# A hybrid recurrent and attention block on one core: buffers, load order and one engine's work moved at five places

## The chip, the cores and the metric

The kernel runs on one core of a Trainium2 chip. The core has TensorE (PE, with PEld for its weight loads), VectorE (DVE), ScalarE (ACT), GpSimd (POOL) and SyncE (SP, which here only issues DMA). The metric is the device time of one execution in microseconds (us), the median of several.

## The reference

One layer, sequence 2048, width 1024, all in float32. From the normed and modulated input h come two branches, merged by gates and projected:

```python
h = rms_norm(x, g_norm) * (1 + scale) + shift          # shift, scale, gate from c
rnn_x, rnn_gate, q, k, v, attn_gate, g_rnn, g_attn = split(h @ w_in)   # eight parts of 1024
a = rg_lru(causal_conv(rnn_x)) * silu(rnn_gate)         # recurrence along the sequence
b = mixture([dilated_window_attention(rope(q), rope(k), v, w, d)
             for w, d in ((128, 1), (512, 4), (2048, 16))]) * silu(attn_gate)
merged = sigmoid(g_rnn) * (a @ w_out_rnn) + sigmoid(g_attn) * (b @ w_out_attn)
out = rms_norm(x + gate * (merged @ w_o), g_final)
```

The rotary angle acts on 32 of the 128 channels of each head ("rotated" rows); the other 96 are "plain".

## The kernel before

Every float32 operand is split into a high and a low part (`hi_act` on ScalarE, `lo_dve` or `lo_pool` on VectorE or GpSimd: low = value − high), and every product is three matmuls (`mm3`). A matmul of 128x512 is the unit nearly everywhere.

The sequence runs in two halves, f = 0 and 1. In each half the input projections are computed in pairs of tiles: `strassen` makes one pair from seven products of 12 matmuls, with weight combinations that are built in the first half, kept in DRAM (`sD`) and read back in the second. The combinations of partial products are kept in the tiles u1, u2 and u3 (u1 a copy by ScalarE, L384; u2 and u3 sums by VectorE, L385 and L390), which lie in the pool that the caller passes: `rp` while the recurrent and gate pairs run, `qp` while the rotated and plain q and k pairs run. `rp` closes when the former are done and `qp` takes its memory.

The order is written out by hand: after each product the functions due at that count run (`later(d, fn)` and `after_prod`, by `run_late`), under a manual schedule, so every engine's stream is in that order. Loads go out on SP, a few on ACT; raw weights pass through a ring R of five tiles (`raw_tile`), in which the weights of the first half, and in the second half those of the output projections, land and are split. In both halves `rotary_tables` builds cosines and sines in pieces: a repeat (L1020), four transposes on TensorE (L1025), a copy or a product (L1031), and a store to the DRAM tensor `tabD`; the repeat and the product use the tag `ev` of `rp`, three buffers, which the gate pairs use too. `load_tables` (L1053) brings them back at the start of `qp` as Ct and St. There, in the first half, `next_norm` loads the other half of x (L511) and squares it (L1240), and `next_even` builds the next operands.

Behind both halves come the attention of eight heads and, between its steps, the output projections' products ("fill"): job j, tile t = 8j + m, eight inputs k of 512 columns each, loaded by `load_y` and split by `split_y`. `at(s, place, fn)` puts a step of a head at a slot of the schedule; a head's queries and keys arrive by four calls of `load_kq` (L1368, L1369), are split by `split_kq` at slots of their own (`enlist`) and the queries are rounded (L1382). From t = 40 on (`TAIL0`), the final projection's operand B is also built on the side: `load_rows` brings rows of w_o, `gate_rows` (L1857) multiplies them by the residual gate, `high`, `low` and `combine` make the operands B11 to T4, in four blocks k by `build_rows`. Then the final product runs in pairs again, with the residual and the last norm behind it.

A DMA's completion is signalled by one of eight semaphores, taken in turn by SP and ACT (DMAHW0 to DMAHW7 in the listings below).

## Time and profile before

| | us |
|---|---|
| median of 3 runs | 2223.52 (2220.85 to 2224.8) |
| the profiled execution | 2226.09 |
| its span | 2224.3 |
| TensorE busy | 2170.7 (98%) |
| VectorE busy | 1443.0 (65%) |
| ScalarE busy | 1287.1 (58%) |
| GpSimd busy | 1027.7 (46%) |
| mean granted TensorE clock | 0.992 |

Times within the span are counted from its start. By them the first half's pairs in `rp` end near 595 us, its rotated and plain pairs near 700; the second half's near 1260 and 1377; attention runs to about 1914, the building of the final operand to about 2050. A row of the timeline is start, duration, engine, line, operation, output <- inputs, shape, count, and in brackets the engine's idle time before it and what ended it.

### The profile page before, as it was taken

To read this page: it belongs to the slowest core of one execution; us is meant where nothing else is said; L and a number is where in the kernel's file an instruction comes from. 1 tells how busy PE (TensorE), PEld (TensorE's weight loads), DVE (VectorE), ACT (ScalarE), POOL (GpSimd) and SP (SyncE) were. 2 spreads that over 40 slices of the span, in tenths; PEclk is the share of its full clock that TensorE was granted. 3 is DMA by queue.
4 is the path that set the end of the run, shared out by engine and by line. 5 is a ranking of instruction groups with operands and counts; after the bars stand their busy time and mean duration, and the time that the engine had idled before them with its cause. 6 is when DMAs were issued, how large, how long until landed. Compare 5 with 4: busy or idle time off the path is not lost.

```text
span 2224.3 us, 34201 instructions
## 1 busy us (share of the span) xinstructions
PE 2170.7 (98%) x11326; PEld 1836.2 (83%) x11326; DVE 1443.0 (65%) x2518; ACT 1287.1 (58%) x2570; POOL 1027.7 (46%) x764
## 2 busy tenths in 40 slices
PE   8999999999999999999999999999999999999998
PEld 5998888888777998888788887788888988887886
DVE  5838888878546715544435353466777777688787
ACT  6637678668543626557447311677888887433333
POOL 2457777667557422222223112455666664310443
PEclk9999999999999999999999999999999999999999
DMA  8367887887989468898888998877887886898543
GB/s 286 117 214 256 281 294 270 295 286 263 316 274 293 129 211 271 291 290 270 295 285 305 341 338 260 267 242 250 269 269 219 249 247 217 297 318 282 180 166 109
DMA packets 412278, 573.41 MB, mean 258 GB/s; under 512 B 72423, under 2 KB 270275, under 8 KB 411077
## 3 DMA queue, kind: packets, MB, share of 16 engines
q1 hardware_dynamic: 369892, 442.82, 63.5%
q10 hardware_dynamic: 42016, 128.36, 15.1%
q8 instruction: 90, 1.47, 0.3%
q14 instruction: 88, 0.71, 0.1%
q0 software_dynamic: 192, 0.05, 0.0%
HBM read 352.99 MB, written 218.11 MB: 257 GB/s over the span
## 4 chain that ended last, share of the span: by engine, by line
PE 53%; DMA 5%; issue 3%; DVE 3%; ACT 3%; POOL 2%; SPq 1%; ACTq 0%; POOLq 0%; DVEq 0%
PE pj L150 10%; PE X L150 10%; PE V L150 9%; PE W L150 5%; PE Z L150 5%; PE Y L150 4%; PE sc L150 3%; PE o L150 3%; PE pg L150 1%; PE pT L1505 1%; PE pT L1518 1%; ACT pp L1421 1%; DMA S<-wD 1%; POOL q L1382 1%; POOL kq L164 1%
## 5 line engine op out<-in xcount | busy, mean ns | idle before, releaser
L164 POOL TENSOR_TENSOR S<-R,S 128x512 fp32r<-128x512 f32 x168 | 257.8, 1542 | 170.4 <-ACT S L158 70.0
L150 PE MATMUL X<-T,S 128*128 128x512 f32 x1344 | 325.9, 391 | 6.3 <-ACT u L384 4.7
L150 PE MATMUL pj<-yh,S 128*128 128x512 f32 x896 | 327.2, 406 | 4.2 <-ACT yh L158 1.5
L150 PE MATMUL V<-T,S 128*128 128x512 f32 x1344 | 324.9, 391 | 2.3 <-DVE t L454 2.0
L150 PEld LDWEIGHTS X<-T,S 128*128 128x128 f32 x1344 | 252.5, 189 | 61.8 <-ACT u L384 6.5
L150 PEld LDWEIGHTS V<-T,S 128*128 128x128 f32 x1344 | 251.6, 188 | 57.6 <-DVE t L454 3.3
L150 PEld LDWEIGHTS pj<-yh,S 128*128 128x128 f32 x896 | 169.4, 189 | 36.1 <-DVE S L167 2.2
L164 POOL TENSOR_TENSOR S<-s,S 128x512 fp32r<-128x512 f32 x92 | 140.1, 1523 | 115.2 <-ACT S L158 69.1
L150 PE MATMUL pj<-yl,S 128*128 128x512 f32 x448 | 177.0, 395 | 3.2 <-DVE yl L167 3.0
L1421 ACT ACTIVATE pp<-pp,st 128x256 f32<-128x256 f32 (+3 forms) x256 | 133.5, 523 | 59.8 <-DVE st L1420 59.2
L150 PE MATMUL Y<-T,S 128*128 128x512 f32 x672 | 163.4, 392 | 0.0
L150 PE MATMUL Z<-T,S 128*128 128x512 f32 x672 | 161.9, 390 | 0.0
L150 PE MATMUL W<-T,S 128*128 128x512 f32 x672 | 161.7, 389 | 0.0
L150 PEld LDWEIGHTS Y<-T,S 128*128 128x128 f32 x672 | 127.0, 189 | 26.4
L150 PEld LDWEIGHTS W<-T,S 128*128 128x128 f32 x672 | 126.0, 188 | 27.0 <-issue 0.9
L167 DVE TENSOR_TENSOR ptl<-pT,pth 128x384 fp32r<-128x384 f32 (+1 forms) x160 | 97.9, 628 | 77.2 <-ACT pth L158 75.0
L150 PEld LDWEIGHTS Z<-T,S 128*128 128x128 f32 x672 | 125.9, 188 | 26.1
L164 POOL TENSOR_TENSOR s<-R,s 128x512 fp32r<-128x512 f32 x32 | 45.8, 1430 | 208.4 <-ACT s L158 161.8
L912 DVE SCALAR_TENSOR_TENSOR xc<-xr,par,xc 128x512 f32<-128x512 f32 x96 | 99.0, 1031 | 47.9 <-ACT xc L906 45.6
L158 ACT ACTIVATE S<-R 128x512 fp32r<-128x512 f32 x168 | 101.5, 622 | 46.8 <-DMA R<-in_w_in_dram 14.2
L1485 ACT ACTIVATE pp<-pp,M 128x256 f32<-128x256 f32 (+3 forms) x256 | 118.0, 523 | 9.7 <-DVE M L1608 9.7
L1420 DVE CUSTOM_DVE_ANT_0 pp<-sc,msk 128x256 f32<-128x256 f32 (+3 forms) x256 | 103.6, 448 | 29.0 <-PE sc L150 27.1
(416 smaller groups left out, 4927.1 us busy)
## 6 DMA issues: line engine op xcount, KB each, us to landing
sD<-S ACTq DMA_DIRECT2D x196, 512.0 KB, 4.2
S<-sD SPq DMA_DIRECT2D x196, 512.0 KB, 5.3
S<-wD SPq DMA_DIRECT2D x82, 512.0 KB, 5.3
R<-in_w_in_dram SPq DMA_DIRECT2D x136, 256.0 KB, 4.3
wD<-s ACTq DMA_DIRECT2D x64, 256.0 KB, 5.4
T<-in_w_mod_dram SPq DMA_DIRECT2D x8, 1024.0 KB, 11.7
vN<-ev SPq DMA_DIRECT2D x64, 128.0 KB, 2.8
zaT<-ev SPq DMA_DIRECT2D x32, 256.0 KB, 4.4
```

The lines of the kernel that those rows point to most:

```text
L150: nc.tensor.matmul(o, lhsT=l, rhs=r, start=st, stop=sp, **kw)
L158: nc.scalar.activation(o, i, AF.Copy)
L164: nc.gpsimd.tensor_tensor(o, i, h.bitcast(F32), ALU.subtract)
L167: return nc.vector.tensor_tensor(o, i, h.bitcast(F32), ALU.subtract).ins
L912: nc.vector.scalar_tensor_tensor(xc, xr[:, i : i + CH], cw(i), xc, ALU.mult, ALU.add)
L1382: nc.gpsimd.tensor_copy(t[:, l], src.rearrange("p r (b a) -> p b r a", b=4))
L1420: nc.vector.tensor_tensor_reduce(pdst, s_ps, mask, 1.0, 3e38, ALU.add, ALU.min, m_)
L1421: nc.scalar.activation(pdst, pdst, AF.Exp, bias=m_, scale=-1.0, accum_out=l_)
L1485: nc.scalar.activation(pp, pp, AF.Copy, scale=w)
L1505: nc.tensor.transpose(pt[:, c0 + j * P : c0 + (j + 1) * P], pp[i][:, k * P : (k + 1) * P], ident)
L1518: nc.tensor.transpose(pt[:, c * P : (c + 1) * P], pp[:, half * P : (half + 1) * P], ident)
```

## The change

Five edits. (1) u1, u2 and u3 lie in a pool `pu` that is opened before `rp` and closed after `qp`, in each half. With it the table loads, the x loads of `next_norm`, and the steps behind them are put off by one to three products. (2) In the second half the tables' repeat and result tiles come from the ring R. (3) The first head's four key loads are called at one slot. (4) The inputs 5 to 7 of the sixth job (t = 40 on) are loaded into the last quarters of operand tiles that are not yet built, as the later jobs' inputs are already; for that the rest of job 5's steps runs behind the opening of the pool `fp`, and one weight split moves from k = 2 to k = 5. (5) The rows of w_o are multiplied by the gate on VectorE, in halves of 512 columns.

```diff
-    def strassen(up, f, key, done):
+    def strassen(f, key, done):
+        up = pu[0]
...
-        strassen(rp, f, ("r", m), done)
+        strassen(f, ("r", m), done)
...
             def repeat():
-                v["rep"] = T(rp, [P, 4, 8, 16], F32, "ev", bufs=3)
+                v["rep"] = raw_tile([P, 4, 8, 16]) if f else T(rp, [P, 4, 8, 16], F32, "ev", bufs=3)
...
             def store():
-                t = T(rp, [P, CH], F32, "ev", bufs=3)
+                t = raw_tile([P, CH]) if f else T(rp, [P, CH], F32, "ev", bufs=3)
...
     def load_tables(qp, f):
...
-            nc.sync.dma_start(t[:], tabD[f, i])
+            later(1 + i, lambda i=i, t=t: nc.sync.dma_start(t[:], tabD[f, i]))
...
     def next_norm():
-        xs = load_x(xp, 2, "x", 2)
+        xs = []
+        later(3, lambda: xs.extend(load_x(xp, 2, "x", 2)))
...
         for r in range(4):
-            later(5 + r, lambda r=r: square(r))
-            later(12 + r, lambda r=r: nc.scalar.activation(xs[r], xs[r], AF.Copy, scale=ss[:, 1, r : r + 1]))
-        later(9, lambda: rstd_first(ss))
-        later(10, lambda: rstd_last(ss))
+            later(7 + r, lambda r=r: square(r))
+            later(14 + r, lambda r=r: nc.scalar.activation(xs[r], xs[r], AF.Copy, scale=ss[:, 1, r : r + 1]))
+        later(11, lambda: rstd_first(ss))
+        later(12, lambda: rstd_last(ss))
...
+        pu[0] = pools.open("pu", bufs=1)
         rp = pools.open("rp", bufs=1)
...
-        touch = [T(qp, [P, CH], F32, tag, bufs=n) for tag, n in (("t0", NT0[f]), ("t1", NT1), ("u1", 1), ("u2", 2), ("u3", 1))]
+        touch = [T(qp, [P, CH], F32, tag, bufs=n) for tag, n in (("t0", NT0[f]), ("t1", NT1))]
...
-        pools.close("qp")
+        pools.close("qp", "pu")
...
         def enlist(self, B):
             for c, (ld, s, place) in enumerate(((5, 2, HEAD), (5, 2, SOFTMAX), (4, 1, HEAD), (3, 0, HEAD))):
-                at(B - ld, TAIL, self.load_kq, c)
+                at(B - (ld if B else 5), TAIL, self.load_kq, c)
...
         def load_y(j, k, t):
-                if t >= TAIL0:
+                if t >= TAIL0 or j == NB + 1 and k > KH:
...
-                if k % KH == 2 and x >= 2 * TAIL0:
+                if k == 5 and t == TAIL0:
+                    split_w(x + 1)
+                if k % KH == 2 and x > 2 * TAIL0:
                     split_w(x + 2)
...
-        owed = spend(fill, TAIL0 * KT - n_steps[0], 0)
     pools.close("ap", "sc", "pT", "po")

     fp = pools.open("fp", bufs=1)
...
+    with tc.manual_schedule():
+        spend(fill, TAIL0 * KT - n_steps[0], 0)
...
-    def gate_rows(k, i):
-        nc.gpsimd.tensor_tensor(v[k, i][:], v[k, i][:], v["gate"][:], ALU.mult)
+    def gate_rows(k, i, j):
+        t = v[k, i][:, j * CH : (j + 1) * CH]
+        tt(t, t, v["gate"][:, j * CH : (j + 1) * CH], ALU.mult)
...
-            (0, gate_rows, k, 0), (6, gate_rows, k, 1), (6, high, "B11", k), (7, low, "B11", k, lo_dve),
+            (0, gate_rows, k, 0, 0), (2, gate_rows, k, 0, 1), (4, gate_rows, k, 1, 0), (6, gate_rows, k, 1, 1), (6, high, "B11", k), (7, low, "B11", k, lo_dve),
```

Below the edit's line in the listing all line numbers of the changed kernel are higher (by one at L384, by five at L1857).

ScalarE at the first half's passage from `rp` to `qp`, before: the copy u of the first rotated pair and what stands around it (sD is the store of a weight combination, S a split weight).

```order
L158 ACTIVATE S_1008_5817<-R_968_5588 128x512 [waits PE_49]
L276 DMA sD<-S_992_5751 128x1024 [waits DMAHW5_49,Pool_49]
L158 ACTIVATE S_1010_5834<-s_981_5682 128x512 [waits DMAHW2_49,DVE_49,PE_49]
L276 DMA sD<-S_995_5774 128x1024 [waits DMAHW6_49,Pool_49]
L384 ACTIVATE u_1012_5841<-X_5803 128x512 [waits DMAHW4_49,PE_49]
L158 ACTIVATE S_1017_5862<-R_986_5709 128x512 [waits DMAHW1_49,DMAHW0_49]
```

And in the changed kernel:

```order
L158 ACTIVATE S_1003_5812<-R_968_5591 128x512 [waits PE_49]
L276 DMA sD<-S_992_5754 128x1024 [waits DMAHW5_49,Pool_49]
L158 ACTIVATE S_1005_5830<-s_981_5685 128x512 [waits DMAHW2_49,DVE_49,PE_49]
L276 DMA sD<-S_995_5777 128x1024 [waits DMAHW6_49,Pool_49]
L385 ACTIVATE u_1007_5837<-X_5797 128x512 [waits PE_49]
L158 ACTIVATE S_1014_5862<-R_986_5712 128x512 [waits DMAHW1_49,DMAHW0_49]
```

The copy keeps its place and no longer waits for a DMA.

SP ahead of the first head, before: msk is the mask, kraw the keys and queries of one of four parts, fg a gate tile of the fill, S one of its weights.

```order
L1332 DMA msk_12722<-in_cst_dram 128x896 [waits DMAHW1_49,PE_49]
L1368 DMA kraw_12768<-kT 128x256 [waits DMAHW2_49]
L1369 DMA kraw_12768<-qT 128x256 [waits DMAHW3_49]
L1368 DMA kraw_12771<-kT 128x256 [waits DMAHW4_49,DVE_49,Pool_49]
L1369 DMA kraw_12771<-qT 128x256 [waits DMAHW5_49]
L1710 DMA fg_12777<-grT 128x512 [waits DMAHW6_49,PE_49]
L1368 DMA kraw_12785<-kT 128x256 [waits DMAHW7_49]
L1369 DMA kraw_12785<-qT 128x256 [waits DMAHW0_49]
L340 DMA S_2216_12788<-wD 128x1024 [waits DMAHW1_49,PE_49]
L1368 DMA kraw_12799<-kT 128x256 [waits DMAHW2_49]
L1369 DMA kraw_12799<-qT 128x256 [waits DMAHW3_49]
L340 DMA S_2219_12810<-wD 128x1024 [waits DMAHW4_49,PE_49]
```

And in the changed kernel:

```order
L1333 DMA msk_12724<-in_cst_dram 128x896 [waits DMAHW1_49,PE_49]
L1369 DMA kraw_12770<-kT 128x256 [waits DMAHW2_49]
L1370 DMA kraw_12770<-qT 128x256 [waits DMAHW3_49]
L1369 DMA kraw_12773<-kT 128x256 [waits DMAHW4_49,DVE_49,Pool_49]
L1370 DMA kraw_12773<-qT 128x256 [waits DMAHW5_49]
L1369 DMA kraw_12776<-kT 128x256 [waits DMAHW6_49]
L1370 DMA kraw_12776<-qT 128x256 [waits DMAHW7_49]
L1369 DMA kraw_12779<-kT 128x256 [waits DMAHW0_49]
L1370 DMA kraw_12779<-qT 128x256 [waits DMAHW1_49]
L1711 DMA fg_12785<-grT 128x512 [waits DMAHW2_49,PE_49]
L340 DMA S_2211_12793<-wD 128x1024 [waits DMAHW3_49,PE_49]
L340 DMA S_2213_12812<-wD 128x1024 [waits DMAHW4_49,PE_49]
```

fg and the first S moved behind the eight key loads; the last key load waits on DMAHW1, which msk's completion holds.

VectorE in the last of the four blocks, before: R is the evicted product, yl the low part of a next input, S and st split weights, B11l the low part of an operand.

```order
L1716 TENSOR_TENSOR R_3914_21026<-pj_20952,fg_20944 128x512 [waits DMAHW4_49,PE_49]
L1718 TENSOR_TENSOR R_3914_21026<-R_3914_21026,fg_20946 128x512 [waits DMAHW5_49,DVE_49]
L167 TENSOR_TENSOR yl_21033<-T4l_20190,yh_21032 128x512 [waits DMAHW1_49,Activation_49]
L167 TENSOR_TENSOR st_3889_20925<-st_3889_20925 128x512 [waits DMAHW2_49,Activation_49]
L167 TENSOR_TENSOR st_3895_20957<-st_3895_20957 128x512 [waits DMAHW6_49,Activation_49]
L1716 TENSOR_TENSOR R_3924_21075<-pj_21016,fg_21009 128x512 [waits DMAHW1_49,PE_49]
L1718 TENSOR_TENSOR R_3924_21075<-R_3924_21075,fg_21011 128x512 [waits DMAHW3_49,DVE_49]
L167 TENSOR_TENSOR S_3903_20990<-S_3903_20990 128x512 [waits DMAHW7_49,Activation_49]
L167 TENSOR_TENSOR S_3913_21024<-S_3913_21024 128x512 [waits DMAHW5_49,Activation_49]
L1716 TENSOR_TENSOR R_3930_21117<-pj_21069,fg_21060 128x512 [waits DMAHW0_49,PE_49]
```

And in the changed kernel:

```order
L1717 TENSOR_TENSOR R_3905_21034<-pj_20960,fg_20952 128x512 [waits DMAHW4_49,PE_49]
L1719 TENSOR_TENSOR R_3905_21034<-R_3905_21034,fg_20954 128x512 [waits DMAHW5_49,DVE_49]
L167 TENSOR_TENSOR yl_21041<-T4l_20159,yh_21040 128x512 [waits DMAHW1_49,Activation_49]
L167 TENSOR_TENSOR st_3880_20933<-st_3880_20933 128x512 [waits DMAHW2_49,Activation_49]
L167 TENSOR_TENSOR st_3886_20965<-st_3886_20965 128x512 [waits DMAHW6_49,Activation_49]
L1717 TENSOR_TENSOR R_3915_21083<-pj_21024,fg_21017 128x512 [waits DMAHW2_49,PE_49]
L1719 TENSOR_TENSOR R_3915_21083<-R_3915_21083,fg_21019 128x512 [waits DMAHW3_49,DVE_49]
L167 TENSOR_TENSOR S_3894_20998<-S_3894_20998 128x512 [waits DMAHW7_49,Activation_49]
L167 TENSOR_TENSOR S_3904_21032<-S_3904_21032 128x512 [waits DMAHW5_49,Activation_49]
L1862 TENSOR_TENSOR st_3908_21055<-st_3908_21055,st_3775_20246 128x512 [waits DMAHW0_49]
L1862 TENSOR_TENSOR st_3908_21055<-st_3908_21055,st_3775_20246 128x512
L1717 TENSOR_TENSOR R_3921_21126<-pj_21077,fg_21068 128x512 [waits DMAHW0_49,PE_49]
```

The gate halves (L1862) stand behind the split of T4l and two evictions, ahead of a third eviction, and the first of them waits for the load of its row.

More of the change, by code (lines that the diff above doesn't have):

```diff
@@ L1058, in decoder_block @@
     plain_at = [None]
-    plain_pool = [None]
+    pu = [None]
     NT0, NT1 = (4, 5), 3
@@ L1103, in rotated @@
                 steps_after(n_prod[0], ((2, shuffle), (3 + x, sines), (4 + x, add), (5 + x, store)))
-            strassen(qp, f, (base, "rotated"), rotated)
+            strassen(f, (base, "rotated"), rotated)
             yield
@@ L1133, in plain @@
                     steps_after(n_prod[0], ((wait + 1, store),))
-                strassen(plain_pool[0], f, (base, t), plain)
+                strassen(f, (base, t), plain)
                 yield
@@ L1190, in gate @@
                     steps_after(n_prod[0], ((1, sigmoid), (2, product)))
-                strassen(ep, f, (base, m), gate)
+                strassen(f, (base, m), gate)
                 yield
@@ L1276, in decoder_block @@
         plain = plain_pairs(f)
+        pu[0] = pools.open("pu", bufs=1)
         rp = pools.open("rp", bufs=1)
-        plain_pool[0] = rp
         plain_at[0] = lambda: T(rp, [P, CH], F32, "ev", bufs=3)
@@ L1299, in decoder_block @@
         qp = pools.open("qp", bufs=1)
-        plain_pool[0] = qp
         plain_at[0] = lambda: T(qp, [P, CH], F32, "t0", bufs=NT0[f])
-        touch = [T(qp, [P, CH], F32, tag, bufs=n) for tag, n in (("t0", NT0[f]), ("t1", NT1), ("u1", 1), ("u2", 2), ("u3", 1))]
+        touch = [T(qp, [P, CH], F32, tag, bufs=n) for tag, n in (("t0", NT0[f]), ("t1", NT1))]
         tabs = load_tables(qp, f)
```

## The prediction

> **What bounds the kernel now.** I read the page's list of engines first, then PE's waits, then windows of 25 us around them, then the timeline at each place.

> ```profile
> PE 2170.7 (98%) x11326; PEld 1836.2 (83%) x11326; DVE 1443.0 (65%) x2518; ACT 1287.1 (58%) x2570; POOL 1027.7 (46%) x764
> PE sc L150 <- POOL q L1382: 8.0, 9, 3.7
> PE pj L150 <- DVE yl L167: 3.0, 3, 2.2
> ```

> TensorE is busy 2170.7 us of a span of 2224.3, so only 53.6 us are idle. The change takes no matmul away; it can act on that idle time and on the clock. The columns of the waits are the sum, the count and the longest. Single stalls of 3.7 and 2.2 us stand out here, and of 3.84 and 2.39 in rows below; the diff touches a buffer or an engine behind each of the four.

> ```profile
> 598.00:601.50 3.50, 2.07 (x5) 1.69 (x6) 1.82 (x2) 1.12 (x2) 1.27 (x1) 0.64 1.03 404
> 600.00:625.00 25.00, 24.91 (x105) 20.19 (x104) 16.22 (x30) 12.28 (x22) 16.28 (x12) 0.95 0.93 321
> 1100.00:1125.00 25.00, 25.00 (x112) 20.67 (x111) 11.26 (x15) 14.50 (x21) 5.23 (x5) 1.00 0.86 282
> 2000.00:2025.00 25.00, 21.39 (x87) 16.60 (x86) 24.86 (x34) 13.28 (x24) 6.64 (x3) 0.95 0.95 319
> 2022.00:2025.60 3.60, 3.56 (x9) 2.79 (x10) 3.56 (x4) 1.78 (x3) 2.35 (x1) 0.54 0.76 208
> ```

> The columns are PE, its weight loads, DVE, ACT, POOL, the granted clock, and the DMA share. An undisturbed window holds 112 matmuls at clock 1.00. Behind the stalls the clock falls too (0.64 at 598, 0.54 at 2022), so a stall costs more than its idle time. How much more is read where a product of 12 matmuls runs right behind one:

> ```profile
> 1089.22 0.66 PE L1025 MATMUL pg<-cs,ev 128*128 128x128 f32 x4 [2.39 <-DVE ev L1020]
> 1089.63 4.58 PE L150 MATMUL Y<-T,S 128*128 128x512 f32 x12
> 1094.05 2.92 PE L150 MATMUL X<-T,S 128*128 128x512 f32 x12
> 717.74 0.66 PE L531 MATMUL pg<-cs,x 128*128 128x128 f32 x4 [1.52 <-DVE hf L548]
> 718.15 1.08 PE L150 MATMUL X<-S,T 128*128 128x256 f32 x7
> ```

> In the undisturbed window a product of 12 takes 25.00 × 12 / 112 = 2.7. Y, behind 2.39 us of idle, holds 4.42 (1089.63 to 1094.05): 1.7 for the clock. Behind 1.52 us of idle at 717.74 the seven half-width matmuls run without such a stretch. So I count about 1.6 us of clock with every stall of 2.2 us or more and none below 1.5; between them I don't know.

> [...]

> **The change part by part.** *Product sums in their own pool (u1, u2, u3).*

> ```profile
> 589.57 2.04 SPq L1188 DMA_DIRECT2D gaT<-ev  x2
> 598.77 0.60 ACT L384 ACTIVATE u<-X 128x512 f32<-128x512 f32 x1 [8.22 <-DMA gaT<-ev]
> 599.43 4.38 PE L150 MATMUL X<-T,S 128*128 128x512 f32 x12 [3.84 <-ACT u L384]
> 603.64 2.89 PE L150 MATMUL Y<-T,S 128*128 128x512 f32 x12
> 595.71 3.33 SPq L511 DMA_DIRECT2D x<-in_x_dram  x2
> 605.07 1.06 ACT L1240 ACTIVATE hf<-x 128x1024 bf16<-128x1024 f32 x1 [1.72 <-DMA x<-in_x_dram]
> 620.22 3.01 PE L150 MATMUL X<-T,S 128*128 128x512 f32 x12
> ```

> The first copy of a finished product in the pool of the rotated pairs sits where the gate rows `ev` lay, and waits for their store: ScalarE idles 8.22 us, TensorE 3.84, and the product behind holds 4.21 instead of 2.7. In a pool that outlives both, the copy waits for TensorE alone. The gross gain is 3.84 + 1.5 = 5.3. What is late next: the x loads now stand behind two input-weight loads on SP, and the squares of x two products later on ScalarE. In before x landed at 605.05 (the square's start), 9.3 us after its issue at 595.71; ScalarE runs in order, so a square that waits holds the next pair's u1. By these rows the squares are through some 10 us behind, at about 615; that product ran at 620.22 and would want to run 5.3 us earlier, at 614.9. So a fraction of the advance is given back. DMA is at 0.93 of its engines from 600 to 625; a stage that waits for weights would give back more. Between 0.5 (nearly all) and 5.3 I take 3.0, the middle. In the second half the same edit meets no stall of TensorE: nothing.

> *Table tiles from the ring of raw weights (second half only).*

> ```profile
> 1081.75 6.96 DMA tabD<-ev
> 1088.73 0.43 DVE L1020 COPY ev<-an 128x512 f32<-128x512 f32 x1 [3.17 <-DMA tabD<-ev]
> 1083.84 1.73 DVE L1184 SCALAR_TENSOR_TENSOR ev<-sg,ev 128x512 f32<-128x512 f32 x1
> ```

> The last repeat waits for the store of a table row out of the same three `ev` buffers, 6.96 us. In the new order it waits for an older raw weight of the ring, read and stored well before, so the copy can follow the operation at 1083.84 at about 1085.6. TensorE is free at 1086.8 (1089.22 less 2.39): the whole 2.39 goes, and its 1.7 of clock: 4.1. Two things may eat into it: the copy needs its raw buffer's store landed, and the table tiles pass as well through a ring of five, so weight loads can be held. Bounds 2.0 and 4.1; I take 4.0, because VectorE has 3.17 idle ahead of the copy and 1.2 is enough.

> *First head's keys.*

> ```profile
> 1385.42 5.86 DMA kraw<-qT
> 1379.52 5.00 DMA msk<-in_cst_dram
> 1384.58 0.32 SPq L340 DMA_DIRECT2D S<-wD  x1
> 1392.07 1.26 POOL L164 TENSOR_TENSOR kq<-kraw,kq 128x512 fp32r<-128x512 f32 x1 [2.27 <-ACT kq L158]
> 1393.27 1.17 POOL L1382 CAST q<-kq 128x512 fp32r<-128x512 f32 x2
> 1393.94 3.06 PE L150 MATMUL sc<-kq,q 128*128 128x128 f32 x12 [3.67 <-POOL q L1382]
> ```

> The fourth key's second load is issued at 1385.42, lands 5.86 later, and split (POOL 1.26), cast (1.17) and scores follow one after another. All eight loads now go out in one row, ahead of an `fg` load and of the weight load at 1384.58. But SP's loads take completion semaphores in turn, eight of them (the listing above shows each waiting for the one eight before it): the last of the eight takes the one that msk holds until 1384.5 (1379.52 + 5.00). So it is issued only 0.9 earlier; as that weight load and `fg` no longer stand ahead of it, its landing should come down from 5.86 towards the 5.00 of msk or below: I let it land 2.2 to 2.5 earlier, near 1388.9. TensorE then starts near 1391.7 instead of 1393.94: 2.2, and with 1.4 of idle left no clock drop, another 1.6; of their 3.8 I take 3.4, since 1.4 lies just under the 1.52 that I know to be free. Below: 0.9 earlier alone, so 1.0; above: the whole 3.67 + 1.6. fg and S land later for it; both are first used behind the scores.

> *Next inputs in unbuilt operands.*

> ```profile
> 1919.33 1.24 SPq L346 DMA_DIRECT2D R<-oT  x2
> 1924.49 0.63 ACT L158 ACTIVATE S<-S 128x512 fp32r<-128x512 f32 x1 [5.76 <-DMA S<-wR]
> 1925.69 0.49 PE L150 MATMUL pj<-yh,S 128*128 128x512 f32 x1 [1.52 <-ACT yh L158]
> 1926.50 0.61 PE L150 MATMUL pj<-yl,S 128*128 128x512 f32 x1 [0.31 <-DVE yl L167]
> ```

> ScalarE holds three input splits behind a weight split that waits 5.76 for its weights; TensorE stands 1.52 + 0.31. The change puts this weight split behind the inputs, and frees the inputs from the ring's buffers. But the last two input loads stay behind the same completion semaphores on SP, so they go out no earlier; and the weight split, three products later, may itself come late. At best 1.83 + 1.6 of clock, less what is left: 3; at worst a weight that comes 1.5 later. I take 0.5.

> *Gated rows on VectorE.*

> ```profile
> L1857 POOL TENSOR_TENSOR st<-st,st x8: 2381/2436/2895, 1933.7 to 2023.3; 128x1024 f32<-128x1024 f32 x8
> 2018.10 2.74 POOL L1857 TENSOR_TENSOR st<-st,st 128x1024 f32<-128x1024 f32 x1 [15.94 <-DVE yl L167]
> 2019.23 2.15 DVE L1718 TENSOR_TENSOR R<-R,fg 128x512 f32<-128x512 f32 x1
> 2021.31 0.68 DVE L167 TENSOR_TENSOR yl<-T4l,yh 128x512 fp32r<-128x512 f32 x1
> 2022.04 0.59 PE L150 MATMUL pj<-yl,S 128*128 128x512 f32 x1 [2.16 <-DVE yl L167]
> ```

> Eight POOL operations of 2.4 to 2.9 us become 16 on VectorE of half their width, as wide as the split of the next inputs there (0.68 at 2021.31): 10.9 us more. But the VectorE operation at 2019.23, with both operands in SBUF and beside the POOL operation, takes 2.15 for this width: 1.46 of stretch. If each of the eight POOL operations meets one such, 11.7 goes (an estimate), and VectorE's load stays even. Where it matters is the order: this stretch of 1.46 stands ahead of the split that TensorE waits for, and in the new order this block's gate halves come behind it. The stall there becomes 2.16 − 1.46 = 0.7, and its 1.7 of clock goes: 3.2. VectorE is full there (24.86 of 25.00), so another split may be late instead. Between 0 and 4 I take 2.5.

> Sum: 3.0 + 4.0 + 3.4 + 0.5 + 2.5 = 13.4 us.

> **The rivals.** *Given back to DMA.* The rotated stage is paced by its transfers (DMA share 1.03 at 598, 0.93 behind it), so part one gives nothing, and the clock drops stay at one of the other places: 0 + 4.0 + 2.2 + 0 + 1.5 = 7.7, 2215.8. For it: that share; against: TensorE is busy 24.91 of 25 us from 600 to 625, so at this share the weights keep up.

> *Everything, and more.* All stalls go with their clock: 5.3 + 4.1 + 5.3 + 3.0 + 3.2 = 20.9, 2203. Against it: the key load's completion semaphore.

> *VectorE waits for the rows (slower).*

> ```profile
> DMA to landing us min/median/max: 5.6/7.4/8.2
> ```

> These are the loads of w_o rows. On POOL their wait held nothing else; on VectorE the gate halves wait in line, and behind them stand evictions and weight splits of the running product. Evened out, each us that a load lands later than before holds VectorE, and then TensorE, up to one us, eight times. With 1.7 us more (9.1 at the median) that is 13.6, the whole gain; with 2.3 more, and one drop of clock of 1.6 in each of four blocks, 18.4 + 6.4 − 13.4 = 11 slower: 2235. No load took over 8.2; so a small chance. [...]

> *It doesn't do what it says.* In the listing the table loads that the diff defers keep their place on SP in the first half, and two of the input loads go out no earlier: that is in the sum already (0 and 0.5). Were the keys' loads held by msk alone, their 3.4 would be the 1.0 of its lower bound: 2212.5, inside the range.

> **How the numbers follow.** The profiled execution took 2226.09 us, 2.6 over the median of 2223.52 (2220.85 to 2224.8), above all three. I take the 13.4 off the median: 2210.1. Chances: forecast 0.63 (the weak keys included), given back 0.17, everything 0.08, VectorE waits 0.06, and 0.06 that gains of several parts fail together and it stays within a few us. A measurement of this kernel can tell about 0.2%, 4.4 us, from no change: faster means below 2219.1. The ends of the parts sum to 2.0 (0.5 + 2.0 + 1.0 − 1.5 + 0) and 21.7 but won't be met all at once; the range reaches 7.1 us below the forecast (2203, the case of everything) and 9.4 above it (2219.5, nearly all of what the small ends would leave). Faster 0.83, same 0.10, slower 0.07.

> **What would show it right or wrong.** Right: no u1 with a wait for gaT; the first product of the rotated pairs 2.7 behind the one before; the table transposes without a stall and clock 1.00 at 1090; the first window's scores 2 us earlier and at clock 1.00; no VectorE operation of 2 us or more between 1930 and 2025; clock 1.00 at 2022. Wrong: a stall of 4 to 5 us between 605 and 625 with u1 behind a square of x; the clock still 0.5 behind shorter stalls; a VectorE wait for st<-in_w_o_dram with TensorE waiting for a weight split right behind it.

## The result, and the profile after

| | before | changed |
|---|---|---|
| median, us (6 runs each) | 2224.16 (2220.85 to 2228.09) | 2216.31 (2214.49 to 2218.67) |
| profiled execution, us | 2226.09 | 2214.49 |
| TensorE busy, us | 2170.7 | 2162.3 |
| GpSimd busy, us | 1027.7 | 1003.4 |
| mean granted clock | 0.992 | 0.996 |

The ratio is 0.997 (95% interval 0.9959 to 0.9982): 7.9 us faster at the medians and 6.7 by the ratio, inside the predicted range, but only about half of the 13.4 us forecast. Two later comparisons, beside 34 and 20 runs of before, gave 0.9975 (0.9963 to 0.9986) and 0.998 (0.9969 to 0.9992), that is 5.9 and 5.5 us at the medians. The changed kernel's page, its first part, and PE's waits (sum, count, longest):

```profile
PE 2162.3 (98%) x11326; PEld 1831.0 (83%) x11326; DVE 1439.8 (65%) x2534; ACT 1287.9 (58%) x2570; POOL 1003.4 (45%) x756
```

```profile
PE sc L150 <- POOL q L1383: 5.2, 9, 1.2
PE X L150 <- ACT u L385: 4.3, 3, 3.0
PE pj L150 <- DVE st L1421: 1.9, 1, 1.9
PE pj L150 <- DVE yl L167: 1.5, 3, 0.7
```

Idle time of TensorE went only from 53.6 to 50.4 us; the busy time fell by 8.4, and with the same matmuls that is clock. Before had six drops of the clock behind stalls from 599 on, each 3.41 us at half speed; the changed kernel has one, at 622. Five drops fewer, at 1.7 us each, are 8.5. But the two profiled executions are 11.6 us apart, more than the medians, and part of that is luck: one of the six drops, at 1469, stands at no edit's place, and it is back in the second and third profile of the changed kernel. Place by place, in the timeline (a pair of rows for each edit's place), then the gate halves by their line (shortest, median and longest in ns) and the last window:

```profile
599.11 2.88 PE L150 MATMUL X<-T,S 128*128 128x512 f32 x12
621.42 4.61 PE L150 MATMUL X<-T,S 128*128 128x512 f32 x12 [2.99 <-ACT u L385]
602.04 2.87 SPq L512 DMA_DIRECT2D x<-in_x_dram  x2
611.71 1.06 ACT L1242 ACTIVATE hf<-x 128x1024 bf16<-128x1024 f32 x1 [8.28 <-DMA x<-in_x_dram]
1085.05 0.41 DVE L1021 COPY R<-an 128x512 f32<-128x512 f32 x1
1088.27 3.00 PE L150 MATMUL Y<-T,S 128*128 128x512 f32 x12
1091.11 2.88 PE L150 MATMUL X<-T,S 128*128 128x512 f32 x12
1386.36 0.69 DVE L1717 TENSOR_TENSOR fg<-pj,fg 128x512 f32<-128x512 f32 x1 [10.82 <-DMA fg<-grT]
1387.74 0.47 PE L150 MATMUL pj<-yh,S 128*128 128x512 f32 x1 [1.91 <-DVE st L1421]
1388.51 1.57 PE L150 MATMUL sc<-kq,q 128*128 128x128 f32 x12
2012.06 0.50 PE L150 MATMUL pj<-yl,S 128*128 128x512 f32 x1 [0.72 <-DVE yl L167]
```

```profile
L1862 DVE TENSOR_TENSOR st<-st,st x16: 683/686/693, 1926.1 to 2020.8; 128x512 f32<-128x512 f32 x16
```

```profile
2000.00:2025.00 25.00, 22.99 (x100) 18.21 (x99) 22.48 (x37) 11.84 (x21) 0.00 (x0) 1.00 0.88 286
```

The first rotated product runs on without a stall, and the second pair's waits 2.99, with a drop, behind squares that wait for x. Tables and gated rows are as forecast (Y holds 2.84; stall 0.72; clock 1.00). At the keys the scores no longer wait for the cast; a fill product waits 1.91 for the first softmax step instead, which stands on VectorE behind an eviction that waits 10.82 for its gate tile fg.

### The profile page after: what moved, and what is told of

It is laid out like the page before. It is cut to its first block, busy times and chain, and to the rows that moved or that the text cites. A ratio compares the mean times of both kernels' runs of the same rounds, so it can differ in the third digit from the quotient of the medians.

```text
span 2212.7 us, 34220 instructions
## 1 busy us (share of the span) xinstructions
PE 2162.3 (98%) x11326; PEld 1831.0 (83%) x11326; DVE 1439.8 (65%) x2534; ACT 1287.9 (58%) x2570; POOL 1003.4 (45%) x756
## 4 chain that ended last, share of the span: by engine, by line
PE 54%; DMA 4%; issue 3%; ACT 3%; DVE 2%; POOL 2%; SPq 1%; ACTq 0%; POOLq 0%; DVEq 0%
PE X L150 10%; PE pj L150 10%; PE V L150 9%; PE W L150 5%; PE Z L150 5%; PE Y L150 4%; PE sc L150 3%; PE o L150 3%; PE pg L150 1%; PE pT L1506 1%; DMA vraw<-vN 1%; PE pT L1519 1%; ACT pp L1422 1%; ACT pp L1486 1%; DMA R<-in_w_in_dram 1%
## 5 line engine op out<-in xcount | busy, mean ns | idle before, releaser
L150 PE MATMUL pj<-yh,S 128*128 128x512 f32 x896 | 325.3, 404 | 5.5 <-DVE st L1421 1.9
L150 PE MATMUL X<-T,S 128*128 128x512 f32 x1344 | 326.0, 391 | 4.8 <-ACT u L385 4.3
L164 POOL TENSOR_TENSOR S<-R,S 128x512 fp32r<-128x512 f32 x168 | 252.6, 1512 | 171.4 <-ACT S L158 75.1
L150 PE MATMUL V<-T,S 128*128 128x512 f32 x1344 | 324.4, 390 | 1.9 <-DVE t L455 1.6
L150 PEld LDWEIGHTS X<-T,S 128*128 128x128 f32 x1344 | 252.6, 189 | 60.1 <-ACT u L385 5.6
L150 PEld LDWEIGHTS V<-T,S 128*128 128x128 f32 x1344 | 251.8, 188 | 56.1 <-DVE t L455 2.0
L150 PEld LDWEIGHTS pj<-yh,S 128*128 128x128 f32 x896 | 168.3, 188 | 37.6 <-ACT yh L158 3.3
L164 POOL TENSOR_TENSOR S<-s,S 128x512 fp32r<-128x512 f32 x92 | 140.6, 1528 | 118.0 <-ACT S L158 72.1
L150 PE MATMUL pj<-yl,S 128*128 128x512 f32 x448 | 176.2, 393 | 2.5 <-DVE yl L167 1.5
L150 PE MATMUL Z<-T,S 128*128 128x512 f32 x672 | 162.0, 390 | 0.0
L150 PE MATMUL Y<-T,S 128*128 128x512 f32 x672 | 161.8, 390 | 0.0
L150 PE MATMUL W<-T,S 128*128 128x512 f32 x672 | 161.6, 389 | 0.0
L150 PEld LDWEIGHTS W<-T,S 128*128 128x128 f32 x672 | 126.0, 188 | 27.0 <-issue 0.9
L167 DVE TENSOR_TENSOR ptl<-pT,pth 128x384 fp32r<-128x384 f32 (+1 forms) x160 | 97.9, 629 | 77.2 <-ACT pth L158 75.0
L150 PEld LDWEIGHTS Y<-T,S 128*128 128x128 f32 x672 | 125.9, 188 | 26.1
L150 PEld LDWEIGHTS Z<-T,S 128*128 128x128 f32 x672 | 125.8, 188 | 26.1
L164 POOL TENSOR_TENSOR s<-R,s 128x512 fp32r<-128x512 f32 x32 | 46.7, 1459 | 204.3 <-ACT s L158 184.4
L158 ACT ACTIVATE S<-R 128x512 fp32r<-128x512 f32 x168 | 101.4, 621 | 41.5 <-DMA R<-in_w_in_dram 14.6
L158 ACT ACTIVATE S<-s 128x512 fp32r<-128x512 f32 x100 | 62.3, 623 | 97.2 <-DVE s L285 74.7
## 6 DMA issues: line engine op xcount, KB each, us to landing
T<-in_w_mod_dram SPq DMA_DIRECT2D x8, 1024.0 KB, 11.6
```

The costliest lines, as they stand in the source:

```text
L150: nc.tensor.matmul(o, lhsT=l, rhs=r, start=st, stop=sp, **kw)
L158: nc.scalar.activation(o, i, AF.Copy)
L164: nc.gpsimd.tensor_tensor(o, i, h.bitcast(F32), ALU.subtract)
L167: return nc.vector.tensor_tensor(o, i, h.bitcast(F32), ALU.subtract).ins
```

## The experiments

TensorE runs the same 11326 matmuls in the same order in every kernel here. So a stage can be measured from the start of one matmul to that of another, the same two in each trace. "Stage" below is that: the rotated stage, with the last products ahead of the rotated pairs and the first steps behind the plain ones, is 573.2 to 718.0 in the first profile of before (144.8 us), the tables 1085.3 to 1098.2 (12.9), the first scores 1386.5 to 1400.0 (13.5), the inputs 1921.1 to 1931.9 (10.8), the gated rows 1990.8 to 2027.4 (36.6). Ratios are to before, with intervals.

**The changed kernel again** (no edit).

> The changed kernel once more, for a second profile. Matmul by matmul, the first profile of it ran 3.7 us later than before at the end of the first half's recurrent pairs, ahead of every edit. Theory N (that is chance between executions): a second profile has another value there, between 0 and 4, and the five edits give the same local gains as in the first (sums' pool 2.4, tables 5.0, keys 3.6, inputs 0.8, gated rows 3.1, each within 0.7). Theory S (the new pool's memory costs it): it stays at 3 to 4 us.

Ratio 0.9975. The 3.7 us at the start were chance: the same stretch is back at its length of before here. Tables 8.6, scores 10.3, rotated stage 142.4, as in the first; inputs 13.0 against 10.0 with a clock drop, so this place varies by 3 us in one and the same kernel.

**Undoing edit 1.**

```diff
-        pu[0] = pools.open("pu", bufs=1)
         rp = pools.open("rp", bufs=1)
+        pu[0] = rp
...
         qp = pools.open("qp", bufs=1)
+        pu[0] = qp
```

and the table loads, x loads and squares as before.

> The changed kernel with the product sums in the two working pools again and with the table and x loads and the squares where they were: edits 2 to 5 alone. Theory G (the pool's gain was given back, 2.4 of 5.3 kept): 2 to 3 us slower than the changed kernel, a stall of 3.8 and a clock drop at 599 back, no stall above 0.6 at 620, about 5.5 us faster than before. Theory S (the new pool costs the early stage 3.7): faster than the changed kernel by about 1.

Ratio 0.9973 (0.9962 to 0.9985), median 2215.99 beside 2216.43 for the changed kernel: no worth of edit 1 shows in the time, and theory G's stall of 3.8 did not come back. A reason stands in the trace of this kernel, which has the old wait:

```profile
594.66 0.60 ACT L385 ACTIVATE u<-X 128x512 f32<-128x512 f32 x1 [3.30 <-DMA gaT<-ev]
595.53 2.88 PE L150 MATMUL X<-T,S 128*128 128x512 f32 x12
614.82 3.00 PE L150 MATMUL V<-T,S 128*128 128x512 f32 x12 [2.80 <-DVE t L455]
```

ScalarE waits for the store of gate rows here too, but 3.30 instead of 8.22, and TensorE not at all. The landings of those four stores, in the first profile of before and in this kernel:

```profile
DMA to landing us min/median/max: 4.2/5.9/9.1
```

```profile
DMA to landing us min/median/max: 5.8/5.9/6.2
```

One store of 9.1 us had made the 3.84 us stall of the first profile. The old pools are in nine profiles. In one other, that of the last experiment below, the slowest store took 8.9 and TensorE stalled 3.08, with a drop; in one it took 7.8 and the stall was 1.61; in the other six it took 6.1 to 6.6 and TensorE did not stall. Nor does the stall lengthen the stage: the three with it took 144.8, 143.6 and 141.0 us, the six without it 140.7 (here, the shortest of all) to 146.9.

**Squares later; x earlier.** Two ways to free the second pair's u1, on the changed kernel:

```diff
-            later(7 + r, lambda r=r: square(r))
+            later(10 + r, lambda r=r: square(r))
```

with the scaling and what stands between three products later too;

> The changed kernel with the four squares of x three products later again (10 to 13, scaling 17 to 20), so that they stand behind the second rotated pair's copy u1 on ScalarE. Theory Q (squares that wait for x hold u1): the stall of 2.99 at that pair's product falls under 0.6, its clock drop goes, and the kernel is 3.5 to 4.5 us faster than the changed one. Theory D (the stage is paced by its transfers, and u1 would wait for a store's completion semaphore anyway): the stall stays above 2 us, gain under 1.

and the loads and squares where they were before the change, with the pool kept:

```diff
-            later(7 + r, lambda r=r: square(r))
+            later(5 + r, lambda r=r: square(r))
```

> The changed kernel with the pool kept, but the tables' and x loads and the squares at the places of before. Theory Q: x is issued some 6 us earlier and lands near 605, the squares are through by 613, the second pair's stall falls under 1 and 2 to 4 us are gained on the changed kernel. Theory D: input weights then come later instead, the stall stays above 2 us or shows as a wait for a split weight; gain under 1.

Ratios 0.9981 (0.9971 to 0.999) and 0.9975 (0.9965 to 0.9986): neither is faster than the changed kernel. With the squares later:

```profile
615.03 3.04 PE L150 MATMUL X<-T,S 128*128 128x512 f32 x12 [0.83 <-ACT u L385]
625.17 4.12 PE L150 MATMUL X<-T,S 128*128 128x512 f32 x10 [3.92 <-POOL S L164]
```

Theory Q is right that the squares held u1 (the stall of 2.99 falls to 0.83) and wrong on the time: two products further on a split weight is 3.92 late, with the clock drop. With x earlier the copy u1 holds nothing either, but the product V just ahead waits 2.52 for VectorE. Stages 144.1 and 142.1.

**One edit at a time, on the kernel before.** In this order, the lines of each (for the inputs with the `split_w` and `spend` lines of the change, for the rows with `build_rows`):

```diff
+                v["rep"] = raw_tile([P, 4, 8, 16]) if f else T(rp, [P, 4, 8, 16], F32, "ev", bufs=3)
+                t = raw_tile([P, CH]) if f else T(rp, [P, CH], F32, "ev", bufs=3)
...
+                at(B - (ld if B else 5), TAIL, self.load_kq, c)
...
+                if t >= TAIL0 or j == NB + 1 and k > KH:
...
+        tt(t, t, v["gate"][:, j * CH : (j + 1) * CH], ALU.mult)
```

> The kernel before with edit 2 alone (table tiles from the ring). Theory F (a stall of the first profile is there in every execution): 4 to 5 us faster; its profile shows no stall at 1089, and the stalls of 3.7, 1.8 and 2.2 us with their clock drops at 1394, 1926 and 2022 are all there, since those edits are left out. Theory V (the stalls that end with a landing vary from execution to execution): 2 to 4 us faster, and at least one of the other three is below 1 us or has no clock drop; the stall of 3.84 at 599, also there in this kernel, is another such.

> The kernel before with edit 3 alone (first head's keys at one slot). Theory F: 3.5 us faster, stall before the first scores 1.9 in place of 3.7 without a clock drop, the stalls at 599, 1089, 1926 and 2022 as in the first profile. Theory V: 1 to 3 us faster at the median, the clock drop at the first scores comes and goes, and the stalls at 599 or 1926 are smaller than in the first profile, while that at 1089 stays.

> The kernel before with edit 4 alone (next inputs in unbuilt operands, the weight split moved). Theory F: 0.8 us faster, a single stall of about 0.8 at the place of the two of 1.52 and 0.31. Theory V: no difference within 1 us; the landing of the inputs' loads decides, and a stall of 1 to 3 us with a clock drop can be there with the edit too.

> The kernel before with edit 5 alone (gated rows on VectorE in halves). Theory F: 3 us faster, no VectorE operation over 1.2 us between 1930 and 2025, the stall of 2.16 at 2022 falls to 0.7. Theory V: the stretch goes in every execution, since it hangs on the order of two engines and not on a landing alone, so 2 to 3 us faster here too; the clock drop may instead be found at the stall of 1.3 that stands 7 us ahead, and then the gain is 1.5.

Ratios 0.9996 (0.9981 to 1.001), 0.9992 (0.998 to 1.0004), 1.0003 (0.9985 to 1.002) and 0.9996 (0.9983 to 1.001): no time alone settles anything, at 3 us to either side. The stages do. Theory V holds on the tables, where three of the six profiles without the edit have a drop (12.4 to 12.9 us) and three have none (9.2 to 10.0): with the old buffers the wait for the table's store is always there, but its length and its drop are not. This is the kernel with the inputs' edit alone:

```profile
1076.84 6.24 DMA tabD<-ev
1083.10 0.43 DVE L1020 COPY ev<-an 128x512 f32<-128x512 f32 x1 [2.15 <-DMA tabD<-ev]
1083.58 0.66 PE L1025 MATMUL pg<-cs,ev 128*128 128x128 f32 x4 [0.30 <-DVE ev L1020]
```

The store took 6.24 instead of 6.96 and TensorE stalled 0.30 instead of 2.39, without a drop: a stage of 9.2 against 12.9.

**Before again, and edit 1 alone.**

> The kernel before, once more, for a second profile. Theory V (the first profile of before was one of the long executions: its store of gate rows landed late and each stall drew a clock drop): at most two of the four stalls at 599, 1394, 1926 and 2022 are as long with a drop, and the rotated stage is 1 to 4 us shorter than the 144.8 of the first. Theory F (they are there in every execution): all of them within 0.5 us of the first profile.

> The kernel before with edit 1 alone (sums in their own pool, tables, x and squares put off). Theory P (the rotated stage is paced by its transfers, and the store that held u1 is late only in some executions): no difference within 2 us of before, rotated stage 142 to 144 us as with the two old pools; u1 never waits for gaT. Theory G (part of a steady gain is kept): 2 to 3 us faster.

Before again has a stage of tables of 10.0 (a stall of 1.18, no drop), none at 599, and other stalls in the rotated stage, 143.2 long; the drops at the scores, inputs and gated rows are there. So in these two profiles theory V holds for the first half and the tables, and theory F, nearly, for the rest. At the gated rows it does not hold always: in two of the six profiles without edit 5 the drop fell at the 1.3 us stall ahead, and the stall of 2.16 was 0.58 and 0.59. Edit 1 alone: ratio 1.0008 (0.9997 to 1.002), stage 142.5.

**More traffic in the rotated stage**, on the changed kernel:

```diff
+        for i in range(2):
+            later(13 + i, lambda i=i: nc.sync.dma_start(twice[i].rearrange("j (r d) -> j r d", r=2), xv[2, 2 * i : 2 * i + 2].rearrange("r j d -> j r d")))
```

> The changed kernel with 2 MB more of traffic in the rotated stage: two copies of 1 MB each from x to an unused place in DRAM, behind the x loads. Theory P (paced by transfers): the stage, 142.4 to 142.7 us in two profiles of the changed kernel, grows by 3 to 7 us (2 MB at about 300 GB/s are 6.7) and its stalls name weights or stores. Theory E (the stage's stalls are ScalarE's and VectorE's own, and transfers fill gaps): under 1 us.

Stage 149.1, 6.4 and 6.7 more than in the first two profiles of the changed kernel, 5.1 more than in its third; ratio 1.0007 (0.9994 to 1.002), so the whole gain is gone. The stalls of over 2 us, and the copy of u1 that waits for the added transfer itself:

```profile
651.99 4.58 PE L151 MATMUL V<-T,S 128*128 128x512 f32 x12 [2.55 <-DVE t L456]
670.64 4.40 PE L151 MATMUL X<-T,S 128*128 128x512 f32 x12 [5.59 <-ACT u L386]
640.30 0.60 ACT L386 ACTIVATE u<-X 128x512 f32<-128x512 f32 x1 [2.90 <-DMA twice<-in_x_dram]
```

2 MB cost about what 2 MB take at 300 GB/s (the stage moved 294 in the first profile of before, at a DMA share of 0.92, and 300 in that of the changed kernel, at 0.94), as theory P says, and these transfers did not just fill gaps: theory E is out. So the stage is paced by its transfers, and a stall removed at its head comes back further on. One rival is left: the copies landed after 8.3 us and held completion semaphores that long, as the wait of 2.90 shows, and this run does not separate that from the load on the DMA engines.

**Next inputs on GpSimd**, on the changed kernel:

```diff
-                (lo_dve if k % 2 or j > NB + 1 else lo_pool)(yl[:], t[:], yh[:])
+                (lo_dve if k % 2 else lo_pool)(yl[:], t[:], yh[:])
```

> The changed kernel with every other low part of the next inputs in the last two jobs on GpSimd, which the gated rows have left idle there, in place of VectorE. Theory R (VectorE full at 2000 to 2025 makes the stalls of 1.3 and 0.7 that remain): both go, 2 to 4 us faster in the stage of the gated rows, of 33.1 to 34.7 us in five profiles with edit 5. Theory L (GpSimd's operations stretch VectorE's beside them, 2.15 for 0.68, as the gated rows did): no gain or up to 2 us slower, with VectorE operations of 1.3 us and more back there.

Ratio 0.9999 (0.9987 to 1.0011); the stage of the gated rows 37.6, 3 us over the longest of the 33.1 to 34.7 of every kernel with edit 5 and VectorE's inputs, with a drop of 6.83 us. Theory L:

```profile
2010.69 1.72 POOL L164 TENSOR_TENSOR yl<-T1h,yh 128x512 fp32r<-128x512 f32 x1
2011.20 1.75 DVE L167 TENSOR_TENSOR S<-S 128x512 fp32r<-128x512 f32 x1
2012.37 1.73 POOL L164 TENSOR_TENSOR yl<-T4h,yh 128x512 fp32r<-128x512 f32 x1
2012.88 1.77 DVE L167 TENSOR_TENSOR yl<-T3l,yh 128x512 fp32r<-128x512 f32 x1
2013.01 1.22 PE L150 MATMUL pj<-yh,S 128*128 128x512 f32 x2 [3.44 <-DVE S L167]
```

The VectorE subtraction beside a GpSimd one took 1.75 us, where one at 2001.68, with none beside it, took 0.69; the GpSimd one took 1.72, where the median of GpSimd's 22 of that width in before (yl out of R) is 1.30.

**Three edits** (tables, keys and gated rows on the kernel before), beside **the changed kernel a third time**.

> The kernel before with edits 2, 3 and 5 (tables, keys, gated rows), without the sums' pool and the moved inputs. Theory T (the local gains of these three, 2.4, 2.8 and 2.5 us as means over the profiles, add up, and edits 1 and 4 are worth nothing): 5 to 9 us faster than before, within 2 us of the changed kernel. Theory C (single stalls and clock drops replace one another, so that gains don't add): 1 to 4 us faster than before and slower than the changed kernel by 3 or more.

> The changed kernel on the same chip and beside the same runs of before, for the comparison with the three edits: 6 to 8 us faster than before in both theories; a third profile of it has the table, score and gated-row stages within 0.7 of the first two, and the rotated stage anywhere from 141 to 146.

Ratios 0.9971 (0.996 to 0.9982), median 2214.87, and 0.998 (0.9969 to 0.9992), median 2216.30. The three carry the whole gain, within these intervals; theory T. By their ratios alone the three sum to 3.6 us, with some 5 to either side: the times of the edits alone were too loose to show it.

**The gate tile ahead of the last keys**, on the three edits:

```diff
-                at(B - (ld if B else 5), TAIL, self.load_kq, c)
+                at(B - (ld if B else 5 - (c == 3)), TAIL, self.load_kq, c)
```

> The three edits with the first head's last key loads one slot later, so that the gate tile fg goes out ahead of them. In the three edits' profile VectorE stood 11.2 us for fg at its eviction, and the first softmax step behind it held TensorE 2.9 us. Theory H (fg, put behind the keys by edit 3, is the new wait): fg lands 1 to 1.5 us earlier, that stall falls to 1.4 to 1.9, the stage of the first scores goes from 11.7 (three edits; 10.0 to 10.4 in the changed kernel) to 9.5 to 10.5, about 1 us faster than the three edits. Theory K (the last keys' landing is as late as fg): the stall moves to the scores behind the cast on GpSimd, as before the change, and the stage stays at 10.5 or more.

In the three edits, and then here:

```profile
1384.21 0.69 DVE L1716 TENSOR_TENSOR fg<-pj,fg 128x512 f32<-128x512 f32 x1 [11.20 <-DMA fg<-grT]
1385.54 0.77 PE L150 MATMUL pj<-yh,S 128*128 128x512 f32 x1 [2.92 <-DVE st L1420]
```

```profile
1383.68 0.69 DVE L1716 TENSOR_TENSOR fg<-pj,fg 128x512 f32<-128x512 f32 x1 [8.06 <-DMA fg<-grT]
1388.26 2.00 PE L150 MATMUL sc<-kq,q 128*128 128x128 f32 x12 [0.34 <-POOL q L1382]
```

The wait for fg falls from 11.20 to 8.06 and the stall of 2.92 behind it is gone; a fill product now waits 1.02 for its weight S, and the scores 0.34 for the cast. So fg was the new wait, as theory H says. What the new order is worth is not shown: the stage is 10.0 instead of 11.7, but the three edits' profile has a clock drop there, and the seven profiles with edit 3 and no drop have 9.8 to 10.4 with fg late. In time it cannot be told from the three edits: 2214.74, ratio 0.9968 (0.9956 to 0.9979). These two show no loss against the changed kernel, with fewer edits; that they beat it is not shown, as the intervals overlap.

## Why the prediction missed

The steps against the stages, as means over profiles with and without each edit (from 17 profiles; the rotated stage without the one of more traffic, the scores without the last kernel, the gated rows without the one of inputs on GpSimd):

| edit | forecast | without it | with it | difference |
|---|---|---|---|---|
| sums' pool | 3.0 | 143.3 (140.7 to 146.9), 9 profiles | 143.3 (142.1 to 145.0), 7 | 0.0 |
| tables | 4.0 | 11.1 (9.2 to 12.9), 6 | 8.6 (8.6 to 8.7), 11 | 2.4 |
| keys | 3.4 | 13.5 (12.9 to 14.2), 6 | 10.8 (9.8 to 12.9), 10 | 2.8 |
| inputs | 0.5 | 10.5 (9.3 to 11.4), 8 | 10.7 (9.7 to 13.0), 9 | −0.2 |
| gated rows | 2.5 | 36.4 (35.1 to 38.6), 6 | 33.9 (33.1 to 34.7), 10 | 2.5 |
| sum | 13.4 | | | 7.5 |

- *The clock terms, and the sum as a whole.* "I take the 13.4 off the median" is the step that failed first. Terms read from one execution were taken off a median of executions that do not all have them: the stages measure 7.5. Of the 5.9 us too many, 3.0 are the sums' pool and 1.6 the tables; the first profile of before had a store of 9.1 us and the longest table stage (12.9). The mechanism of idle time and drop was right (clock 0.50 in the 3.41 us behind the stall of 2.16); how often it strikes was never asked. The rule for the drop, "about 1.6 us of clock with every stall of 2.2 us or more and none below 1.5", was wrong both ways: in other profiles a stall of 2.54 drew no drop and one of 1.3 drew one (last section). And beside "the 1.52 that I know to be free" the same profile has another stall of 1.52, ending at 1925.69, with a drop from 1926.74 on. The forecast's own warning was there: that execution lay above all three runs. The number of its drops was no warning, though: the second profile of before spent as long at half clock behind 599, at other places.
- *Sums' pool.* The gross gain of 5.3 was in the profile (counted from the start of the stage, the changed kernel was 5.1 ahead behind that product), and the squares did hold the next u1 (2.99 and a drop). But "a fraction of the advance is given back" should have read all of it, and not for the squares' sake: the rival "given back to DMA" had the mechanism, as the kernel with the squares later and the one with more traffic indicate. Its 7.7 us for the whole came near by luck as well: it had the tables at 4.0, too high, and the keys at 2.2 and the rows at 1.5, too low. The counter-argument, TensorE busy 24.91 of 25 us, did not bear: the same window holds 20.4 to 23.8 in the other 16 profiles. Perhaps the stall ahead of it had let the weights run ahead; that is not shown.
- *Tables.* Right in mechanism and in what is left (8.6 in every profile, no stall); 4.0 is the gain on executions with a drop there (12.4 to 12.9), 2.4 the mean over those with and without.
- *Keys.* The last key's loads were issued behind msk's semaphore, as forecast, and the scores ran earlier, with no drop in seven of ten profiles. "fg and S land later for it; both are first used behind the scores" was wrong for fg: its eviction stands on VectorE ahead of the first softmax step, which made a stall of 1.7 to 2.9 in seven of the ten; in the other three TensorE waited 1.1 to 2.3 for S. The size, 2.8 for 3.4, came near because most of it was the drop: without one the stage is 9.8 to 10.4, with one 11.7 to 12.9.
- *Inputs.* 0.5 forecast, nothing found, within a scatter of 3 us.
- *Gated rows.* Right step by step: no VectorE operation of 2 us left, the stall of 2.16 at 0.72, the gain 2.5 (a mean again, 35.1 to 38.6 without the edit). The slower rival, VectorE waiting for the rows of w_o, showed as waits of 0.49 and 0.93 us that TensorE did not feel:

```profile
1965.24 0.69 DVE L1862 TENSOR_TENSOR st<-st,st 128x512 f32<-128x512 f32 x1 [0.49 <-DMA st<-in_w_o_dram]
1990.35 0.69 DVE L1862 TENSOR_TENSOR st<-st,st 128x512 f32<-128x512 f32 x1 [0.93 <-DMA st<-in_w_o_dram]
```

Open: the edits sum to 7.5 in the stages and to 5.5, 5.9 and 7.9 in the times. Two of the three intervals reach 7.5; the third ends at 6.9. So a further loss of 1 to 2 us is neither shown nor excluded.

## What to carry to other kernels

In this case a stall that ended with a DMA's landing was a draw, and so was the clock drop behind it: before its price from one profile is taken off a median, ask what the same transfers took elsewhere in the trace (a store of 9.1 beside a median of 5.9 is a warning). A stall removed inside a stage that its transfers pace (DMA share 0.92 and 0.94 over the rotated stage in the first profiles of before and of the changed kernel) came back further on; adding traffic there is a quick test of it. When loads are pulled ahead on one queue, follow each load that is pushed back to its first reader, and then to what stands behind that reader on its engine.

## What the chip showed beyond that

- The length of a stall alone did not decide on the clock's drop here. In the first profile of the changed kernel the stall of 1.29 us at 2006.52 drew none (clock 1.00 from 2000 to 2025); in its second profile the same stall drew one, and in the second profile of before a stall of 2.54 drew none:

```profile
2007.83 0.73 PE L150 MATMUL pj<-yh,S 128*128 128x512 f32 x2 [1.29 <-DVE S L167]
```

```profile
2008.00:2012.00 4.00, 4.00 (x11) 3.12 (x12) 3.99 (x7) 2.96 (x6) 0.00 (x0) 0.58 0.99 310
```

```profile
617.02 2.98 PE L150 MATMUL V<-T,S 128*128 128x512 f32 x12 [2.54 <-DVE t L454]
```

```profile
2018.90:2022.31 3.41, 1.25 (x6) 0.75 (x5) 3.38 (x4) 0.00 (x0) 1.94 (x1) 1.00 0.76 285
2022.31:2025.72 3.41, 3.41 (x9) 2.64 (x9) 3.38 (x4) 1.78 (x3) 2.38 (x1) 0.50 0.81 216
```

```profile
612.56:615.98 3.42, 1.92 (x9) 1.26 (x7) 1.62 (x4) 3.42 (x6) 2.77 (x3) 1.00 1.08 328
615.98:619.39 3.41, 2.37 (x10) 1.99 (x11) 2.05 (x4) 3.38 (x8) 3.41 (x3) 1.00 1.08 386
619.39:622.80 3.41, 3.41 (x16) 2.69 (x15) 2.88 (x7) 0.89 (x2) 2.29 (x2) 1.00 0.71 257
```

  The stall of 1.3 us above drew a drop in the four profiles where all idle time of its stretch came to 1.57 to 1.64, and none in twelve where it came to 1.18 to 1.46.
- In the kernel with inputs on GpSimd, VectorE and GpSimd were both slower side by side: a 128x512 subtraction took 1.75 us on VectorE, 1.06 more than alone, and 1.72 on GpSimd, 0.42 more than its median in before.
- One and the same kernel, before, ran 2214.65 to 2232.73 us in 35 runs beside the single edits. An edit of 2 to 3 us needs its stage, not its time.
